# A retention branch projected per head as seven block products, its heads summed in memory token by token

## The chip, the cores and the metric

The kernel runs on one core of a Trainium2 chip. The metric is the device time of one execution in microseconds; lower is better. The core has TensorE (PE in the profile; PEld is its weight load), VectorE (DVE), ScalarE (ACT), GpSimd (POOL) and SyncE (SP). In this kernel SP and POOL issue nearly all DMAs: SP the plain loads, POOL the stores and the DMAs that add to what is in their destination.

## The reference

One decoder layer on 512 tokens of width 1024. A retention branch and a latent attention branch read the same normalised input; each is projected to width 1024 and gated; their sum goes through an output projection into the residual. An MLP and a gated embedding follow. Cut to the branch in question:

```python
rv = rv.reshape(B, S, RET_HEADS, RET_V_DIM)            # 4 heads, 512 values each
ro = retention(rq, rk, rv)
ro = rms_norm(ro, ret_norm.reshape(RET_HEADS, RET_V_DIM)).reshape(B, S, RET_V_W)
a_ret = (ro * jax.nn.silu(rg)) @ w_br                  # (512 x 2048) @ (2048 x 1024)
...
mixed = jax.nn.sigmoid(gr) * a_ret + jax.nn.sigmoid(gm) * a_mla
x = x + mixed @ w_o
```

The norm's factor is one number for each token and head. As `a_ret` is linear in each head, a head's factor may be applied ahead of `w_br` or behind it, and the four heads' shares may be summed in any order.

## The kernel before

All matrices are handled in tiles of 128 partitions. Every operand of a matmul is held as two tiles, a rounded high part and the low remainder, and each product is three matmuls (`mm3`, line 291). `split` (line 301) makes the two parts: a copy on ACT, then a subtraction on DVE. Weights come as chunks of 128 x 1024 from one stream: `prepare` (line 217) issues the load into a raw buffer, and `load_chunk` (line 246) converts it with one ACT copy and one DVE subtraction. There are 6 raw buffers and 3 pairs of converted ones.

The work is a list of steps in TensorE's order (from line 1099). `run_steps` (line 270) converts the weights of the step behind the present one and prepares three steps ahead. TensorE's order is the list's; on the other engines a planner orders the instructions by the list's priority and its own estimate of when each is ready. Each engine works through its own queue in order.

**Seven products.** Some projections are cut into 2 x 2 blocks and done as seven block products instead of eight: the values (`ret_v`, two heads at once), the gates (`ret_gate`, per head) and the MLP's second matrix (`down`). For these (`key[0] == "sw"`) the sums of weight blocks are made by DMA: product 7 loads a block into a raw buffer t and adds another to it with an accumulating DMA from POOL (line 223); once t is converted, product 6 adds a third block to the same t, and product 4 later a fourth. Product 5 is a load and an accumulation in a buffer of its own; products 1, 2 and 3 are plain loads. Products accumulate in PSUM along three chains (`CHAIN`, line 735): 1, 6, 5, 3 on one; 7, 4 on another; 2 alone. The bank is read behind each product, and the next product of the chain is added on top.

**A head of the retention.** The list from line 1195 has, for each of four heads: queries and keys in four steps (`ret_qk`); for heads 0 and 2 the values of this head and the next (14 steps); the gates in seven steps with `ret_scores`, `ret_attend` and `ret_stats` between them; then `ret_gated`, which multiplies the head's output (features on partitions, tokens along the row) by the gate. `ret_factor` (line 847) comes in the following head, behind its first query step: it spreads the norm's factor over the partitions with four transposes (the tile pbo), multiplies the four tiles by it and splits them. Then `branch_r` (line 855) multiplies by `w_br`: 4 chunks a head, each for two of the eight 128-wide slices of the output, with the weights as the stationary operand and the tokens as the 512 columns. Heads 1 and 3 do their own steps around the branch of the head before; in head 2 the branch of head 1 lies between the values' products.

The result of head 0 is stored in memory (`aside`, line 351); those of heads 1 and 2 are added to it by accumulating DMAs from POOL (line 865). Behind the last head, `reload` (line 869) brings the sums, the gated attention share (zm) and the output gates (sgr) back; the rest of the gates is computed (`gate_r`); head 3's branch is added by DVE directly from PSUM (line 867); and `mix` (line 894) gates, adds and splits each of eight tiles for the output projection `wo`.

**Buffers.** `T` gives one of 45 tiles of 128 x 512 (line 55, NDYN), `K` one of 16 longer-lived ones, `B` one of 8 PSUM banks. During the retention 12 of the K tiles hold the operands of products 6, 5 and 3 of the normalised input. The attention's rotary tiles qp have six buffers of their own (line 567).

## Time and profile before

| | us |
|---|---|
| time, median of 3 runs | 1123.46 (1120.56 to 1124.0) |
| time of the profiled execution | 1125.78 |
| span of the profiled execution, first to last instruction | 1124.0 |
| mean granted TensorE clock in it | 0.997 |

A matmul of 512 columns shows as 389 ns on PE, but matmuls overlap: from start to start they are nearer to the pace that the chain of work shows. Busy PE is therefore no measure of its speed, but idle PE is time lost. The chain of work is followed back from the last instruction to what released each step, so a DMA or an ACT copy on it stands for a stretch in which TensorE was waiting or had no time in hand. From the page, the stretches of the span by engine on that chain, and three groups of DMA issues that the change bears on (destination and source, issuer, count, size, median us from issue to landing):

```profile
PE 87%; DVE 4%; DMA 4%; ACT 2%; issue 2%; SPq 0%; ACTq 0%; DVEq 0%; POOLq 0%
...
wr_rg<-wstream SPq DMA_DIRECT2D x20, 512.0 KB, 4.6
...
wr_rg<-wstream POOLq DMA_DIRECT2D x16, 512.0 KB, 7.7
wr_br<-wstream SPq DMA_DIRECT2D x16, 512.0 KB, 3.5
```

A plain load of a weight chunk lands 3.5 to 4.6 us behind its issue; an accumulating one of the same size takes 7.7.

### The profile page before, as it was taken

To read this page: it belongs to the slowest core of one execution; us is meant where nothing else is said; L and a number is where in the kernel's file an instruction comes from. 1 tells how busy PE (TensorE), PEld (TensorE's weight loads), DVE (VectorE), ACT (ScalarE), POOL (GpSimd) and SP (SyncE) were. 2 spreads that over 40 slices of the span, in tenths; PEclk is the share of its full clock that TensorE was granted. 3 is DMA by queue.
4 is the path that set the end of the run, shared out by engine and by line. 5 is a ranking of instruction groups with operands and counts; after the bars stand their busy time and mean duration, and the time that the engine had idled before them with its cause. 6 is when DMAs were issued, how large, how long until landed. Compare 5 with 4: busy or idle time off the path is not lost.

```text
span 1124.0 us, 14722 instructions
## 1 busy us (share of the span) xinstructions
PE 1107.5 (99%) x5549; PEld 939.0 (84%) x5549; DVE 734.9 (65%) x1206; ACT 536.7 (48%) x762; POOL 85.4 (8%) x113
## 2 busy tenths in 40 slices
PE   9999999999999999999999999999999999999998
PEld 7878878888888889888888987888888888888877
DVE  7777677556785836845483678555466666668675
ACT  7457556444465435445443644434443443445542
POOL 0000000001110020031003000010100100101000
PEclk9999999999999999999999999999999999999999
DMA  8133231356786274599529754693855755738501
GB/s 264 59 98 106 67 99 57 128 210 211 190 225 173 87 212 121 135 202 253 137 92 220 223 172 154 196 274 117 171 165 168 176 166 155 186 123 219 146 29 75
DMA packets 59223, 175.97 MB, mean 157 GB/s; under 512 B 7248, under 2 KB 8656, under 8 KB 58896
## 3 DMA queue, kind: packets, MB, share of 16 engines
q1 hardware_dynamic: 45168, 129.66, 33.8%
q0 software_dynamic: 13840, 45.36, 20.9%
q8 instruction: 43, 0.70, 0.2%
q14 instruction: 28, 0.23, 0.1%
q10 hardware_dynamic: 144, 0.03, 0.0%
HBM read 156.92 MB, written 15.99 MB: 154 GB/s over the span
## 4 chain that ended last, share of the span: by engine, by line
PE 87%; DVE 4%; DMA 4%; ACT 2%; issue 2%; SPq 0%; ACTq 0%; DVEq 0%; POOLq 0%
PE up L168 16%; PE dn L168 14%; PE br L168 6%; PE rg L168 5%; PE rv L168 5%; PE pg L168 4%; PE gr L168 4%; PE rq L168 4%; PE rk L168 4%; PE bm L168 4%; PE wo L168 4%; DMA wr_rg<-wstream 4%; PE gm L168 3%; PE ro L168 3%; PE sc L168 2%
## 5 line engine op out<-in xcount | busy, mean ns | idle before, releaser
L168 PE MATMUL dn<-wh_dn,cl 128*128 128x512 f32 x224 | 87.2, 389 | 0.0
L168 PE MATMUL dn<-wh_dn,ch 128*128 128x512 f32 x224 | 87.2, 389 | 0.0
L168 PE MATMUL dn<-wl_dn,ch 128*128 128x512 f32 x224 | 87.1, 389 | 0.0
L261 ACT ACTIVATE wh_dn<-wr_dn 128x1024 fp32r<-128x1024 f32 x32 | 34.0, 1062 | 75.5 <-PE up L168 54.3
L261 ACT ACTIVATE wh_up<-wr_up 128x1024 fp32r<-128x1024 f32 x32 | 33.9, 1061 | 57.4 <-PE up L168 29.3
L265 DVE TENSOR_TENSOR wl_dn<-wr_dn,wh_dn 128x1024 fp32r<-128x1024 f32 x32 | 39.0, 1220 | 27.5 <-ACT wh_dn L261 27.5
L265 DVE TENSOR_TENSOR wl_rg<-wr_rg,wh_rg 128x1024 fp32r<-128x1024 f32 x20 | 24.3, 1223 | 40.7 <-ACT wh_rg L261 40.4
L265 DVE TENSOR_TENSOR wl_up<-wr_up,wh_up 128x1024 fp32r<-128x1024 f32 x32 | 39.1, 1222 | 17.4 <-ACT wh_up L261 17.4
L970 DVE SCALAR_TENSOR_TENSOR f<-up,bcx 128x512 f32<-128x512 f32 x32 | 20.6, 685 | 44.1 <-PE up L168 44.1
L168 PEld LDWEIGHTS dn<-wl_dn,ch 128*128 128x128 f32 x224 | 42.0, 188 | 8.8
L168 PEld LDWEIGHTS dn<-wh_dn,cl 128*128 128x128 f32 x224 | 42.0, 188 | 8.7
L168 PEld LDWEIGHTS dn<-wh_dn,ch 128*128 128x128 f32 x224 | 42.0, 188 | 8.6
L261 ACT ACTIVATE wh_dn<-dr_dn 128x1024 fp32r<-128x1024 f32 x24 | 25.5, 1060 | 42.2 <-PE up L168 29.1
L223 POOL DMA_DIRECT2D dr_dn<-wstream x24 | 21.4, 892 | 306.3 <-DMA dr_dn<-wstream 182.0
L265 DVE TENSOR_TENSOR wl_dn<-dr_dn,wh_dn 128x1024 fp32r<-128x1024 f32 x24 | 29.3, 1222 | 22.4 <-ACT wh_dn L261 22.4
L261 ACT ACTIVATE wh_rv<-wr_rv 128x1024 fp32r<-128x1024 f32 x28 | 29.6, 1058 | 28.7 <-PE rv L168 11.8
L261 ACT ACTIVATE wh_rg<-wr_rg 128x1024 fp32r<-128x1024 f32 x28 | 29.3, 1054 | 28.9 <-DMA wr_rg<-wstream 23.6
L265 DVE TENSOR_TENSOR wl_br<-wr_br,wh_br 128x1024 fp32r<-128x1024 f32 x16 | 19.5, 1219 | 21.6 <-ACT wh_br L261 21.6
L1028 DVE TENSOR_TENSOR d<-d,dn 128x1024 f32<-128x1024 f32 x24 | 29.2, 1219 | 6.5 <-PE dn L168 6.5
L265 DVE TENSOR_TENSOR wl_rv<-wr_rv,wh_rv 128x1024 fp32r<-128x1024 f32 x20 | 24.4, 1223 | 13.6 <-ACT wh_rv L261 13.6
L861 ACT ACTIVATE rt<-br 128x512 f32<-128x512 f32 x24 | 14.3, 596 | 36.1 <-PE br L168 30.9
L644 ACT ACTIVATE p<-p,ng,hr 128x128 f32<-128x128 f32 (+3 forms) x32 | 20.6, 646 | 15.6 <-DVE ng L642 15.5
(1820 smaller groups left out, 3618.9 us busy)
## 6 DMA issues: line engine op xcount, KB each, us to landing
wr_up<-wstream SPq DMA_DIRECT2D x32, 512.0 KB, 4.4
wr_dn<-wstream SPq DMA_DIRECT2D x32, 512.0 KB, 3.4
dr_dn<-wstream POOLq DMA_DIRECT2D x24, 512.0 KB, 7.6
wr_rv<-wstream SPq DMA_DIRECT2D x20, 512.0 KB, 4.1
wr_rg<-wstream SPq DMA_DIRECT2D x20, 512.0 KB, 4.6
wr_rv<-wstream POOLq DMA_DIRECT2D x16, 512.0 KB, 6.1
wr_rg<-wstream POOLq DMA_DIRECT2D x16, 512.0 KB, 7.7
wr_br<-wstream SPq DMA_DIRECT2D x16, 512.0 KB, 3.5
```

The lines of the kernel that those rows point to most:

```text
L168: return tc.keep_in_program_order(nc.tensor.matmul(*a, **k))
L223: nc.gpsimd.dma_start(raw, chunk(("w", blk, kb, fb, c)), accum_op=ALU.add)
L261: i = ACT(hi, raw, AF.Copy, scale=sign)
L265: TT(lo, raw, hi.bitcast(F32), op=ALU.subtract)
L644: ACT(cols[b], cols[b], AF.Exp, bias=ng[:, b:b + 1], scale=d["rq"][:, b], accum_out=sums[:, b:b + 1])
L861: ACT(t, ps, AF.Copy)
L970: STT(u[:, i], ps[:, i], 0.0, V["bcx2"], op0=ALU.max, op1=ALU.mult)
L1028: TT(to, to, dps[p], op=ALU.add if sign > 0 else ALU.subtract)
```

## The change

Each head's branch becomes seven block products. The roles are exchanged: the head's gated output is the stationary operand and the weights are the 512 columns, so the result has tokens on partitions and the output's width along the row. In this layout the norm's factor is one number per partition. It is applied as the scale of the ACT copy that reads PSUM (or, in the last head, of a DVE operation that also adds), with its negative (`nr`) for products 1, 6 and 4. `ret_factor` with its four transposes and multiplications goes.

The weights of a head are four blocks (256 rows x 512 columns each) used as for the other seven-product projections: 5 plain loads and 4 accumulations, 7 conversions. The output tiles are now 128 tokens x 512 and there are eight of them, `ret[b, n]`: four token blocks by two halves of the width. Head 0 stores the results of products 1, 7, 6 and 3 and accumulates those of 2, 5 and 4; heads 1 and 2 accumulate all 14; head 3 adds all 14 on DVE to the reloaded sums.

`branch_operand` makes a product's operand: a difference where the product needs one, then a split. Those of products 1 and 7 are asked for behind the head's gates, the others two products ahead. The products lie between the next head's query and key steps, in all heads.

Since the sums have tokens on partitions, `ret_turn` transposes each of the eight final tiles once, as four 128 x 128 transposes, for the mix.

Buffers: the values of heads 1 and 3 are stored in memory and loaded back (`odd_v`); the head's output is in two tiles with a tag of their own (o2); qp moves into the common ring, which grows from 45 to 47; result tiles come from K; the reloaded output gates come from T.

```diff
-NDYN, NKEEP, NW, NRAW, NDRAW, AHEAD, PREP, EARLY, PAD = 45, 16, 3, 6, 4, 1, 3, 5, 104
+NDYN, NKEEP, NW, NRAW, NDRAW, AHEAD, PREP, EARLY, PAD = 47, 16, 3, 6, 4, 1, 3, 5, 72
...
+                add(("w", ("br", h), kb, fb, 0), "w_br", _rng(h * RV + kb * 256, 256), _rng(fb * S, S))
...
-            t = dyn.tile([P, S], F32R, tag="qp", name=f"qp{gq}{i}", bufs=6)
+            t = dyn.tile([P, S], F32R, tag="t", name=f"qp{gq}{i}")
...
+                    if blk % 10 == 1:
+                        v[j] = split(t, f"rv{q}{blk}{i}")
+                        continue
+                    if blk == 12:
+                        t = T(f"cv{q}{i}_12")
+                        ACT(t, rvps[ch][i], AF.Copy)
+                    v[j] = aside(f"v{q}{j}", t)
+
+    def odd_v(h):
+        for j in range(4):
+            t = T(f"cv{h}{j}")
+            nc.sync.dma_start(t, R[h]["v"][j])
+            R[h]["v"][j] = split(t, f"rv{h}{j}")
...
+        R[h]["nr"] = sm(f"nro{h}", keep=True)
+        TS(R[h]["nr"], R[h]["r"], -1.0, None, op0=ALU.mult)
...
-    def ret_factor(h):
-        d, r = R[h], R[h]["r"]
-        bc = bcast(B(f"pbo{h}"), lambda b: r[:, b:b + 1])
-        for m in range(4):
-            TT(d["og"][m], d["og"][m], bc, op=ALU.mult)
-            new = K if m < 2 and h < RH - 1 else T
-            d["rog"][m] = split(d["og"][m], None, hi=new(f"rog{h}{m}h", F32R), lo=new(f"rog{h}{m}l", F32R))
...
+    def branch_operand(h, p):
+
+        (a, b), lo_, hi_ = R[h]["o"], slice(0, 256), slice(256, 512)
+        if p == 7:
+            R[h]["s"] = T(f"bs{h}")
+        sv = two(R[h]["s"]) if "s" in R[h] else None
+        if p in (1, 2, 4):
+            src = (a if p == 1 else b)[:, :, hi_ if p == 4 else lo_]
+        elif p == 5:
+            src = two(T(f"bt{h}"))
+            TT(src, a[:, :, hi_], b[:, :, hi_], op=ALU.subtract)
+        else:
+            src = sv
+            if p == 7:
+                TT(sv, a[:, :, hi_], a[:, :, lo_], op=ALU.subtract)
+            else:
+                TT(sv, b[:, :, hi_ if p == 6 else lo_], sv, op=ALU.subtract)
+        hi, lo = two(T(f"bx{h}{p}h", F32R)), two(T(f"bx{h}{p}l", F32R))
+        split(src, None, hi=hi, lo=lo)
+        R[h]["x", p] = [(hi[:, k], lo[:, k]) for k in range(2)]
...
+    def branch_r(w, h, p):
+
+        ch, d = CHAIN[p], R[h]
+        if p in (1, 7, 2):
+            brps[ch] = [B(f"br{h}{p}{i}") for i in range(2)]
+        for k in range(2):
+            for i in range(2):
+                mm3(brps[ch][i], cut(d["x", p][k], i * P), cut(w, k * S, S), p in (1, 7, 2) and k == 0, k == 1,
+                    skip_group_check=True)
+        to, f = {1: (11, "nr"), 7: (22, "r"), 6: (21, "nr"), 2: (11, "r"), 5: (22, "r"), 4: (21, "nr"), 3: (12, "r")}[p]
         for i in range(2):
...
+            b, n = 2 * (to // 10 - 1) + i, to % 10 - 1
+            r, ps = d[f][:, b:b + 1], brps[ch][i]
+            if h == RH - 1:
+                STT(ret[b, n], ps, r, ret[b, n], op0=ALU.mult, op1=ALU.add)
+                continue
+            t = K(f"rt{h}{p}{i}")
+            ACT(t, ps, AF.Copy, scale=r)
+            if h == 0 and p in (1, 7, 6, 3):
+                ret[b, n] = aside(f"ret{b}{n}", t)
             else:
-                TT(ret[n], ret[n], ps, op=ALU.add)
+                nc.gpsimd.dma_start(ret[b, n], t, accum_op=ALU.add)
...
+    def ret_turn(n):
+
+        trp[n] = B(f"tr{n}")
+        for b in range(4):
+            MM(trp[n][:, b * P:b * P + P], ret[b, n // 4][:, n % 4 * P:n % 4 * P + P], ident, is_transpose=True,
+               start=b == 0, stop=b == 3, skip_group_check=True)
...
-        TT(ret[n], ret[n], sgr[n], op=ALU.mult)
-        TT(ret[n], ret[n], zm[n], op=ALU.add)
-        mixed[n] = split(ret[n], f"mix{n}")
+        TT(sgr[n], trp[n], sgr[n], op=ALU.mult)
+        TT(sgr[n], sgr[n], zm[n], op=ALU.add)
+        mixed[n] = split(sgr[n], f"mix{n}")
...
+        qk("rq", 0)()
+        if h:
+            branch_steps(h - 1, [1, qk("rq", 1), 7, 2, qk("rk", 0), 6, 5, qk("rk", 1), 3, 4])
...
+        if h % 2:
+            step(None, odd_v, h)
...
         step(None, ret_gated, h)
+        for p in (1, 7):
+            step(None, branch_operand, h, p)
+    step(None, ret_back)
     for n in range(8):
         step(None, reload, n)
...
+    step(("gr", 5), gate_r, 5)
+    branch_steps(RH - 1, [1, 7, lambda: step(("gr", 6), gate_r, 6), 2, 6, 5, 4, 3])
+    for n in range(4):
+        step(None, ret_turn, n)
+        step(None, mix, n)
+    step(("gr", 7), gate_r, 7)
+    for n in range(4, 8):
+        step(None, ret_turn, n)
+        step(None, mix, n)
```

`ret_back` is eight loads on SP into K tiles; `branch_steps` lists the products and asks for each operand two products ahead.

76 lines of the change are left out of this document (35 added, 41 removed).

## The prediction

> **What bounds the kernel now.** I read the busy times first, then the chain of work that ended last, then the windows of the retention stage. The page's busy times, and from its third part the two large DMA queues:
>
> ```profile
> PE 1107.5 (99%) x5549; PEld 939.0 (84%) x5549; DVE 734.9 (65%) x1206; ACT 536.7 (48%) x762; POOL 85.4 (8%) x113
> ...
> q1 hardware_dynamic: 45168, 129.66, 33.8%
> q0 software_dynamic: 13840, 45.36, 20.9%
> ```
>
> TensorE is idle for only 1124.0 - 1107.5 = 16.5 us of the span. So a matmul less is time won, as long as everything that feeds TensorE stays ahead of it. The chain of work that ended last (start, length, what) gives the pace of the pieces that the change touches; the last but two lines are from the same chain, asked for the end of head 3:
>
> ```profile
> 396.97 21.76 PE br L168 x96
> ...
> 1060.83 1.75 PE tr L168 x16
> ...
> 647.36 5.46 PE gr L168 x24
> 652.82 0.44 PE pbo L168 x4
> ```
>
> 96 matmuls of 512 columns take 21.76 us, so one takes 0.2267 us. Sixteen 128x128 transposes take 1.75 us, so one takes 0.109 us. The four transposes that spread a head's factor (pbo) hold TensorE for 0.44 us. Where TensorE did wait, in the middle of heads 0 and 2, the chain of head 0 reads:
>
> ```profile
> 324.66 4.58 DMA wr_rg<-wstream
> 329.79 8.53 DMA wr_rg<-wstream
> 338.43 1.07 ACT wh_rg L261
> 339.52 1.24 DVE wl_rg L265
> 341.04 6.83 DMA wr_rg<-wstream
> ```
>
> This is one raw weight buffer used four times in series: a load, an accumulating DMA for product 7, a conversion on ACT and DVE, the accumulating DMA for product 6, and so on. The windows (us; busy of PE, PEld, DVE, ACT, POOL with counts; clock; DMA share; GB/s) show what surrounds it:
>
> ```profile
> 322.80:359.00 36.20, 34.57 (x204) 30.45 (x203) 24.21 (x32) 18.28 (x27) 3.44 (x4) 1.00 0.76 203
> 451.40:485.00 33.60, 33.60 (x151) 27.79 (x150) 25.15 (x42) 14.92 (x20) 4.31 (x5) 1.00 0.59 145
> 485.00:540.00 55.00, 55.00 (x267) 46.51 (x266) 27.49 (x29) 26.62 (x35) 12.10 (x14) 1.00 0.98 238
> 540.00:553.40 13.40, 10.84 (x80) 10.23 (x78) 8.35 (x14) 7.08 (x12) 0.86 (x1) 1.00 0.38 96
> 380.60:418.70 38.10, 38.10 (x171) 31.52 (x170) 22.41 (x31) 15.74 (x22) 6.47 (x10) 1.00 0.57 169
> 645.00:692.00 47.00, 46.45 (x216) 38.54 (x215) 38.68 (x65) 19.93 (x28) 0.00 (x0) 1.00 0.45 149
> ```
>
> TensorE loses 36.20 - 34.57 = 1.6 us in head 0 and 13.40 - 10.84 = 2.6 us in head 2, the latter after 55 us in which the DMA engines were at 0.98. So the retention stage is bound by TensorE, with the DMA engines close behind in the even heads, and DVE close behind at the very end (38.68 of 47 us).
>
> **The change part by part.** Durations are of the profiled execution (span 1124.0, its own time 1125.78); the sum is a difference, and I apply it to the median 1123.46.
>
> *Products.* A head's branch took 8 outputs x 4 x 3 = 96 matmuls of 512 columns. Seven products of 2 x 2 x 3 make 84. Four heads: 48 x 0.2267 = **-10.9 us**. The pbo transposes go: 4 x 0.44 = **-1.8**. The turn adds 8 x 4 transposes at 0.109: **+3.5**. TensorE alone: **-9.1 us**. All of it is on the path, since nothing hides a busy TensorE. The Trainium skill (TensorE: Matmul & The Clock Gate, Wait — 56ns, not 53.3ns?) gives 215.7 ns between warm matmuls of 512 columns; this trace has 226.7 at a granted clock of 1.00, and the trace decides. By the page the first term would be -10.4.
>
> *Waits between products.* Product 5 accumulates onto the banks of product 6 directly behind it, so its first matmuls wait until both banks are read. The same turn stands once in the trace, in the value projection (TensorE's timeline):
>
> ```profile
> 322.63 0.39 PE L168 MATMUL rv<-wh_rv,s61h 128*128 128x512 f32 x1
> 323.03 0.51 PE L168 MATMUL rv<-wh_rv,s50l 128*128 128x512 f32 x1
> 323.55 0.50 PE L168 MATMUL rv<-wl_rv,s50h 128*128 128x512 f32 x1
> 323.89 0.39 PE L168 MATMUL rv<-wh_rv,s50h 128*128 128x512 f32 x1
> ```
>
> Three steps took 1.26 us instead of 0.68: 0.58 us. Four heads: **+2.3**. Bounds: 0 (copies at once, the gap being something else) and 5 (two reads behind a 1.07 us conversion each time). A late conversion of wl_rv ends at the same place, so the row is an upper reading for ACT; in head 3 DVE does the reading and is fuller.
>
> *Operands and conversions.* Per head three more weight blocks are converted (1.07 ACT, 1.24 DVE), six more results leave PSUM, the four multiplications by the factor go, and there are seven splits and four differences instead of four splits. In heads 1 to 3 the queries and keys that now lie between the products had 22.41 us of DVE in 38.10 (380.60 to 418.70); with 3 x 1.14 for conversions, and some 2 to 4 us for operands and the second head's values, some 29 in 35. TensorE covers it, 5.44 us for each rq or rk step. If that cover went, 7 us per head would show; I take 0.
>
> *The end.* Here DVE decides. Its timeline:
>
> ```profile
> 649.86 1.22 DVE L265 TENSOR_TENSOR wl_gr<-wr_gr,wh_gr 128x1024 fp32r<-128x1024 f32 x1
> ...
> 676.99 1.22 DVE L265 TENSOR_TENSOR wl_o<-wr_o,wh_o 128x1024 fp32r<-128x1024 f32 x1
> 678.12 0.68 DVE L307 TENSOR_TENSOR mix2l<-re,mix2h 128x512 fp32r<-128x512 f32 x1
> 678.73 0.68 DVE L898 TENSOR_TENSOR re<-re,ze 128x512 f32<-128x512 f32 x1
> 679.33 0.68 DVE L867 TENSOR_TENSOR re<-re,br 128x512 f32<-128x512 f32 x1
> ...
> 691.40 0.68 DVE L307 TENSOR_TENSOR mix7l<-re,mix7h 128x512 fp32r<-128x512 f32 x1
> ```
>
> From start to start a 512-wide operation takes 0.60 us, a conversion 1.14. From 649.9 to the last mix at 692 DVE had 4 + 4 + 8 + 24 operations of 0.60 and 8 conversions of 1.14: 33 us in 42. After the change: 7 splits and 4 differences, 14 accumulations, 24 of the mix (49 x 0.60) and 12 conversions (13.7): 43 us. TensorE reaches the matmul that needs the last mix at 647.36 + 3 x 5.44 + 7 x 2.72 + 3.5 + 5.44 + 2.0 = 693.7, so DVE has 43.8 us for 43, and each instruction that it waits for counts. It sat idle for 9 us before; I allow 3, hence **+2.5** (0 to 6). Behind a DVE that waits stand the splits that the next product needs.
>
> *DMA.* The rates come from the queue rows: 129.66 MB in 0.338 x 1124 us of all sixteen engines is 1.54 us per 512 KB load. On q0 29 plain stores of 256 KB at that pace are 22 us of 235; the other 37.7 MB are accumulating, 2.95 us per 512 KB. A head's branch now needs 5 loads and 4 accumulations instead of 4 loads (+13.3 us), and 14 results for memory instead of 8 (+8.9 where all accumulate); an even head also stores four value tiles (+3.1). Head 2 gets 25.3 us more. From 451.4 to 553.4 the engines were free for 0.41 x 33.6 + 0.02 x 55 + 0.62 x 13.4 = 23 us. So it is nearly full, and the serial chain of the gate weights at its end, which already stalls, becomes later: **+1.5** in head 0 (the value stores fall on it) and **+1.5** in head 2. Bounds 0 and 9 together: none of it in the way, or head 2 full and late by 5.4 us (25.3 less 23, plus the 3.1 that TensorE saves) with 3.1 from the stores in head 0. The result tiles have 4 of 16 keep buffers (12 hold the operands of products 6, 5 and 3), each reused after two products and one rq or rk step of TensorE (2 x 2.72 + 5.44 = 10.9 us). Their DMAs (issue rows of the rt tile):
>
> ```profile
> L861 ACT ACTIVATE rt<-br x24: 580/598/600, 400.1 to 614.8; 128x512 f32<-128x512 f32 x24
> ...
> DMA to landing us min/median/max: 2.3/6.2/10.6
> ```
>
> 0.6 + 0.9 of issue + 6.2 fits; the maximum doesn't, by 1.2 us. When it doesn't, ACT stands at the copy with the conversions behind it, and on POOL the weights' accumulations queue behind the results'. **+1.5** for heads 1 to 3 (0 to 6). The Trainium skill (DMA: Bandwidth & Descriptors, Issuing engines are not separate DMA queues) says that DMAs of all issuers run on the same 16 engines and interleave. That speaks against the change: the accumulations on POOL would not be beside SP's loads but among them. By it the sum is at worst that of the DMA rival below; were POOL's queue a way of its own, the 3.0 and 1.5 of this part would be 0. The 0.98 of 485 to 540, where both queues ran, fits the Trainium skill's sentence.
>
> *Attention.* qp moves from 6 buffers of its own into the common ring, 45 to 47, where 4 or more qp live: two fewer for the rest. The ring was full once (DVE's waits, 45 to 236 us):
>
> ```profile
> DVE o L557 <- DMA zm5d<-zm: 2.2, 1, 2.2
> ```
>
> **+0.5** (-1 to 3). *Reloads.* SP's 8 loads of the sums stand ahead of those of zm, 16 keep buffers for 16 tiles instead of 21; weights queued behind them wait no longer than before: 0 (-1 to 1).
>
> **Sum:** -9.1 + 2.3 + 2.5 + 3.0 + 1.5 + 0.5 = +0.7 us, so **1124 us**: what TensorE saves is given back in small waits.
>
> **The rivals.** *Faster:* the waits are hidden. For it: 55 us at a DMA share of 0.98 passed without one PE stall, and raw buffers run several steps ahead. Then the 6-to-5 wait and one or two us at the end remain: -9.1 + 2.3 + 1.8 = -5, **1118.5**; with nothing at all, 1114. *Slower, by DMA:* in head 2, from the first branch product to the last gate product, accumulations of results and of weights share POOL's queue and the engines. It decides once the DMA share stays at 1.0 beyond 540: 5.4 us late in head 2, 3.1 in head 0 and some 2 each in heads 1 and 3 in place of the 4.5 taken: +9, **1132**. Against it: result tiles aren't urgent. *Slower, by DVE at the end:* if DVE idles 9 us there as before, mixes come 8 us late: 5.5 more than taken, **1130**. *The saving isn't there:* the products are fewer by count, so only a slower matmul could do this; no row suggests it.
>
> **How the numbers follow.** Forecast, no change: 0.38, 1120 to 1127. Faster: 0.32. Slower by DMA: 0.19; slower by DVE at the end: 0.11. A measurement of this kernel tells about 0.3% (3.4 us) from no change; faster is below 1120.1, slower above 1126.8. Range 1113 (nothing in the way) to 1134 (one slow case with a little of the other).
>
> **What would show it.** Right: 5549 - 48 + 16 = 5517 matmuls, PE busy near 1098, PE idle grown by some 10 us at the 6-to-5 turns, the gate products of heads 0 and 2, and ahead of wo. Wrong: idle as before (16 us) means that the waits were hidden; DMA waits inside the branch products mean the DMA rival; a span grown in 45 to 236 us means that the ring of tiles mattered.

## The result: 5% slower, and the profile after

| | before | after |
|---|---|---|
| time, median of 4 runs (us) | 1123.73 | 1181.9 (1180.92 to 1183.23) |
| ratio to before, 95% interval | | 1.0522 (1.0497 to 1.0547) |
| span of the profiled execution (us) | 1124.0 | 1180.0 |
| mean granted TensorE clock in it | 0.997 | 0.978 |

The forecast was 1124 us, with a range from 1113 to 1134. The change costs 58 us.

From the page of the kernel after, the busy times and the two large DMA queues:

```profile
PE 1108.7 (94%) x5517; PEld 935.3 (79%) x5517; DVE 761.1 (64%) x1224; ACT 567.9 (48%) x808; POOL 120.6 (10%) x155
...
q1 hardware_dynamic: 46896, 133.85, 33.4%
q0 software_dynamic: 19376, 60.56, 26.8%
```

The 5517 matmuls are those that were foreseen. TensorE was idle for 16.5 us before; now it is idle for 1180.0 - 1108.7 = 71.3 us. That is 54.8 of the 56.0 us by which the span grew. The other 1.2 us hide two things that nearly cancel. The work got 9.1 us less, by the prediction's count, so busy PE should have come to 1098.4; the remaining 10.3 us are matmuls that took longer at a lower granted clock. They show where the count did not change. All matmuls of the gates (first line, tile rg) and of the output projection (second line, tile wo), us and count behind the length of the window, then granted clock, DMA share and GB/s; before:

```profile
0.00:1200.00 1200.00, 83.50 (x672) 1.00 0.52 147
...
0.00:1200.00 1200.00, 43.98 (x192) 1.00 0.52 147
```

and after:

```profile
0.00:1200.00 1200.00, 88.25 (x672) 0.98 0.60 163
...
0.00:1200.00 1200.00, 46.25 (x192) 0.98 0.60 163
```

The same 672 matmuls take 4.75 us more and the same 192 take 2.27 more; with the values (tile rv, 77.71 to 81.27) that makes 10.6 us.

What TensorE waited for longest, after (tile it was about to write, who released it; us in total, times, longest):

```profile
PE rg L167 <- ACT z L741: 34.4, 2, 17.6
PE rv L167 <- ACT wh_rv L260: 4.6, 1, 4.6
PE wo L167 <- DVE wl_o L264: 4.6, 1, 4.6
```

Two waits are the larger half of the loss: 34.4 us, in the gates of heads 1 and 3. Product 6 of a gate adds onto the banks of product 1, so it must wait until ACT has copied them out (the tile z). No such row stood in the kernel before. Why is a copy of 0.6 us late by 17 us? ACT's timeline of head 1, after, answers it (start, length, line, what, and in brackets the idle time ahead of it with its releaser):

```profile
420.82 0.69 ACT L904 ACTIVATE rt<-br,nro 128x512 f32<-128x512 f32 x1 [4.47 <-DMA ret21d<-rt]
423.00 0.69 ACT L904 ACTIVATE rt<-br,nro 128x512 f32<-128x512 f32 x1 [1.49 <-DMA ret31d<-rt]
423.59 1.05 ACT L260 ACTIVATE wh_rg<-wr_rg 128x1024 fp32r<-128x1024 f32 x1
424.54 0.62 ACT L305 ACTIVATE rv10h<-cv 128x512 fp32r<-128x512 f32 x1
433.86 1.06 ACT L260 ACTIVATE wh_rg<-wr_rg 128x1024 fp32r<-128x1024 f32 x1 [8.70 <-DMA wr_rg<-wstream]
434.82 0.61 ACT L305 ACTIVATE rv11h<-cv 128x512 fp32r<-128x512 f32 x1
435.34 1.04 ACT L260 ACTIVATE wh_rg<-wr_rg 128x1024 fp32r<-128x1024 f32 x1
436.29 0.61 ACT L305 ACTIVATE rv12h<-cv 128x512 fp32r<-128x512 f32 x1
442.06 1.06 ACT L260 ACTIVATE wh_rg<-wr_rg 128x1024 fp32r<-128x1024 f32 x1 [5.16 <-DMA wr_rg<-wstream]
444.65 0.63 ACT L305 ACTIVATE rv13h<-cv 128x512 fp32r<-128x512 f32 x1 [1.53 <-DMA cv<-v03d]
445.18 1.07 ACT L741 ACTIVATE z<-rg 128x512 f32<-128x512 f32 x2
```

The rows show a queue in which one urgent instruction stands last. TensorE had finished product 2 by 429 and needed z. But the planner had put z behind the splits of the reloaded values (rv10h to rv13h), and between these lie the conversions of the gate's products 6, 5 and 4. Two of the conversions and the last split wait for transfers (8.70, 5.16 and 1.53 us), so ACT stood still, with z in its queue. In the kernel before, the two copies stood directly behind the conversions of products 2 and 6, and nothing that waits for a transfer came between; ACT's timeline of head 1, before:

```profile
419.31 1.05 ACT L261 ACTIVATE wh_rg<-wr_rg 128x1024 fp32r<-128x1024 f32 x1
421.69 0.60 ACT L742 ACTIVATE z<-rg 128x512 f32<-128x512 f32 x1 [1.33 <-issue]
422.19 1.05 ACT L261 ACTIVATE wh_rg<-wr_rg 128x1024 fp32r<-128x1024 f32 x1
424.52 0.60 ACT L742 ACTIVATE z<-rg 128x512 f32<-128x512 f32 x1 [1.29 <-PE rg L168]
```

The first of these transfers was late itself. POOL's timeline in the same stretch, after:

```profile
421.81 0.89 POOL L908 DMA_DIRECT2D ret20d<-rt  x1 [6.07 <-ACT rt L904]
423.99 0.87 POOL L908 DMA_DIRECT2D ret30d<-rt  x1 [1.29 <-ACT rt L904]
424.55 1.22 POOL L222 DMA_DIRECT2D wr_rg<-wstream  x1
436.47 0.86 POOL L222 DMA_DIRECT2D wr_rg<-wstream  x1 [10.70 <-DVE wl_rg L264]
```

The sum of weights for product 6 (424.55) was issued behind two accumulations of results. These waited for ACT's copies at 420.82 and 423.00, which had waited for a free result tile, that is, for earlier accumulations to land (4.47 and 1.49 us, first lines of ACT's rows). So one late tile passed through three queues.

What a long wait costs beyond itself, in windows of 10 us, after (length; busy and count of PE, PEld, DVE, ACT, POOL; clock; DMA share; GB/s), and TensorE's first matmuls behind it:

```profile
430.00:440.00 10.00, 0.00 (x0) 0.00 (x0) 3.56 (x4) 3.04 (x4) 0.86 (x1) 0.62 0.50 121
440.00:450.00 10.00, 4.18 (x22) 4.19 (x23) 5.64 (x10) 4.01 (x7) 0.86 (x1) 0.53 0.71 185
```

```profile
427.12 0.28 PE L167 MATMUL rg<-xn7h,wl_rg 128*128 128x256 f32 x1
427.24 0.28 PE L167 MATMUL rg<-xn7l,wh_rg 128*128 128x256 f32 x1
...
445.81 0.58 PE L167 MATMUL rg<-s60h,wl_rg 128*128 128x256 f32 x1 [16.74 <-ACT z L741]
446.19 0.41 PE L167 MATMUL rg<-s60l,wh_rg 128*128 128x256 f32 x1
446.41 0.41 PE L167 MATMUL rg<-s60h,wh_rg 128*128 128x256 f32 x1
```

Ahead of the wait a matmul of 256 columns started every 0.12 us; behind it one every 0.21 to 0.22, at a granted clock of 0.53. The Trainium skill (TensorE: Matmul & The Clock Gate, What's actually happening) says that an idle window of about 3.4 us brings the clock to half; this trace agrees, with 0.53 behind an idle time of 16.74 us. In the same trace 4.60 us were enough: behind the wait for wl_o in the list above, matmuls of 512 columns started every 0.43 us (742.24, 742.67), and later every 0.23 (747.36, 747.59).

### The profile page after: what moved, and what is told of

The parts are those of the page before. It is cut to its first block, busy times and chain, and to the rows that moved or that the text cites. A ratio compares the mean times of both kernels' runs of the same rounds, so it can differ in the third digit from the quotient of the medians.

```text
span 1180.0 us, 14846 instructions
## 1 busy us (share of the span) xinstructions
PE 1108.7 (94%) x5517; PEld 935.3 (79%) x5517; DVE 761.1 (64%) x1224; ACT 567.9 (48%) x808; POOL 120.6 (10%) x155
## 5 line engine op out<-in xcount | busy, mean ns | idle before, releaser
L260 ACT ACTIVATE wh_br<-wr_br 128x1024 fp32r<-128x1024 f32 x28 | 29.6, 1058 | 21.2 <-DMA wr_br<-wstream 12.5
L167 PE MATMUL rg<-s60h,wl_rg 128*128 128x256 f32 x16 | 5.9, 367 | 34.4 <-ACT z L741 34.4
L167 PEld LDWEIGHTS rg<-s60h,wl_rg 128*128 128x128 f32 x16 | 4.1, 256 | 34.8 <-ACT z L741 34.8
```

The costliest lines, as they stand in the source:

```text
L167: return tc.keep_in_program_order(nc.tensor.matmul(*a, **k))
L260: i = ACT(hi, raw, AF.Copy, scale=sign)
```

## The experiments

The theories at the start. **Order:** instructions that TensorE waits for stand in ACT's and DVE's queues behind ones that wait for transfers, because the planner fixes the order ahead of time. **Transfers:** the added traffic fills the DMA engines, and everything comes late, in whatever order. **Tiles:** result tiles and attention tiles share too few buffers. **End:** DVE's work between the last product and the output projection. The first four runs:

*1. The values of heads 1 and 3 asked for earlier, ahead of the head's first query step.*

```diff
+        if h % 2:
+            step(None, odd_v, h)
         qk("rq", 0)()
...
-        if h % 2:
-            step(None, odd_v, h)
```

> The reload and split of an odd head's values (odd_v) is listed ahead of the head's first query step instead of behind its last key step. Theory Q (order of ACT's queue): in heads 1 and 3 the copies of the first gate products (z) stand in ACT's queue behind the conversions of gate products 6, 5, 4 and behind the values' splits; with the step moved they stand ahead of them. Q expects the two waits of 17 us of PE rg for ACT z (34.4 us together) to fall under 2 us each, the granted clock to stay at 1.00 there (about 8 us more), and a time of 1137 to 1146. Theory D (the DMA engines are full, and TensorE would wait for the gate weights anyway): the wait moves from z to the conversions of rg, and the time stays above 1165.

1175.66 us, ratio 1.0468 (1.0407 to 1.0529). The waits for z fell to 0.7 us, as the order theory had it, but the time missed its range of 1137 to 1146. TensorE now waited at another place (waits of this run):

```profile
PE br L167 <- DVE bx22l L306: 10.6, 1, 10.6
PE br L167 <- DVE bx02l L306: 7.9, 1, 7.9
```

The operands of product 2 stood behind the values' splits, whose loads were late again (SP issued them behind weight loads that waited for raw buffers). The wait moved with the splits, and not to the gate weights, where the theory of transfers put it. That speaks for order; but the time is above 1165, where that theory put it too, so moving the splits settles little.

*2. Heads 1 and 3 use the values of the head before; the reload and the splits are left out, the stores stay.*

```diff
-            step(None, odd_v, h)
+            step(None, lambda h=h: R[h].update(v=R[h - 1]["v"]))
```

> Heads 1 and 3 use the values of the head before, so their reload (8 loads) and their splits are left out; the stores of the values stay. Q expects the same as with the step moved, 1135 to 1145, as nothing of the step stands in ACT's queue. If the reload itself (its DMAs, ACT and DVE work) were the cost rather than its place, this is faster than the moved step by more than 10 us. D expects above 1165.

1157.06 us (one run). No wait for z is left, but 15.0 us of waits of gate products for their weights (wl_rg), two of them long, both at product 6 of heads 1 and 3. That is the second half of the mechanism, the sums behind the results in POOL's queue, without the first. The time lies in neither expected range, and 18.6 us below run 1: by the expectation, what costs is the reload itself with its splits, and not only its place.

*3. The 28 accumulating transfers of heads 1 and 2 are left out, the values are as in the changed kernel.*

```diff
-            else:
+            elif h == 0:
                 nc.gpsimd.dma_start(ret[b, n], t, accum_op=ALU.add)
```

> The 28 accumulating DMAs of the results of heads 1 and 2 are left out (so their shares are missing from the sum); everything else, the values' step included, stays. Theory D expects the waits of 17 us in heads 1 and 3 to go in head 3 (whose stage carries head 2's results), stay in head 1 (head 0's results are still stored), and head 2's idle in 500 to 550 us (about 14 us with the slow clock) to go: 1140 or less. Q alone expects head 3's wait to stay at 10 us or more, as ACT's order is the same, and the time at 1160 to 1175.

1169.18 us (one run), waits for z still 27.6 us. Without these 28 transfers most of the long waiting stays, as the order theory expected, so they are not its main cause. They cost some 12 us all the same. The waits for z are 6.8 us shorter, and in head 2, from 500 to 560 us, TensorE is 5.0 us busier, in the changed kernel first and then in this run:

```profile
500.00:560.00 60.00, 52.75 (x214) 41.33 (x213) 29.20 (x33) 27.30 (x36) 16.93 (x20) 0.94 1.01 243
```

```profile
500.00:560.00 60.00, 57.74 (x268) 47.65 (x267) 31.56 (x34) 29.76 (x38) 10.88 (x14) 0.97 0.89 222
```

In that stretch the DMA engines of the changed kernel are full (1.01) and TensorE is idle for 7.25 us: there the theory of transfers holds.

*4. The kernel before, with only the attention's qp tiles moved into the common ring of 47.*

```diff
-NDYN, NKEEP, NW, NRAW, NDRAW, AHEAD, PREP, EARLY, PAD = 45, 16, 3, 6, 4, 1, 3, 5, 104
+NDYN, NKEEP, NW, NRAW, NDRAW, AHEAD, PREP, EARLY, PAD = 47, 16, 3, 6, 4, 1, 3, 5, 104
...
-            t = dyn.tile([P, S], F32R, tag="qp", name=f"qp{gq}{i}", bufs=6)
+            t = dyn.tile([P, S], F32R, tag="t", name=f"qp{gq}{i}")
```

> The kernel before with one part of the change alone: qp in the common ring, which goes from 45 to 47 tiles. From 45 to 236 us TensorE idled about 3 us longer in the changed kernel. If the ring is the cause, this is 2 to 5 us slower than before; if that came from elsewhere (another plan of the order), within 1 us.

1127.95 us, ratio 1.0033 (1.0007 to 1.0058): by that ratio the ring alone costs 3.7 us. The window from 50 to 250 us of the kernel before, and of this one:

```profile
50.00:250.00 200.00, 195.45 (x1082) 166.06 (x1081) 140.14 (x374) 112.28 (x226) 7.77 (x14) 1.00 0.33 107
```

```profile
50.00:250.00 200.00, 192.18 (x1059) 163.12 (x1058) 136.44 (x368) 108.78 (x222) 7.23 (x13) 0.99 0.33 101
```

TensorE loses 3.3 us there, and as much in the changed kernel (192.11 busy).

*5 to 8, one set.* First the values split at once and kept, with nothing left out; then the same with the result tiles taken from the common ring:

```diff
-                    if blk % 10 == 1:
-                        v[j] = split(t, f"rv{q}{blk}{i}")
-                        continue
...
-                    v[j] = aside(f"v{q}{j}", t)
+                    v[j] = split(t, f"rv{q}{blk}{i}")
...
-        if h % 2:
-            step(None, odd_v, h)
```

> The values of heads 1 and 3 are split at once and kept on the chip, as in the kernel before; nothing else is taken back. If ScalarE's order decides (the values' splits ahead of the gate's result copies in its queue), the two long waits of the gate in heads 1 and 3 fall from 34.4 to below 5 us, and a wait of gate products for their weights of about 13 us stays, as when heads 1 and 3 used the values of the head before: 1152 to 1162. If it is only the work of the values (loads and splits) and not its place, the same time. If the two waits come from transfers and not from the order, they stay: 1170 to 1180. If the kept values crowd the common ring, new waits on its tiles: over 1165.

```diff
-            t = K(f"rt{h}{p}{i}")
+            t = T(f"rt{h}{p}{i}")
```

> As the run with the values kept, and the scaled block results are taken from the common ring of 47 tiles in place of the kept ones, of which 4 are free. If the gate weights' sums are late because POOL's queue holds accumulations of results that wait for one of those 4 buffers, the wait of gate products for their weights (13.6 us in two places) falls below 4: 10 to 14 below the run with the values kept, 1142 to 1150. If they are late because the transfers themselves fill the DMA engines, no more than 3 below it. If the ring gets short, other operands come late and it is slower than it.

Kept values: 1164.44 us, ratio 1.0376 (1.0323 to 1.0428). With the results in the ring too: 1150.12, ratio 1.0265 (1.0217 to 1.0313). The first wait is from the run with the values kept, the next two from the run with both:

```profile
PE rg L167 <- DVE wl_rg L264: 13.3, 3, 7.7
```

```profile
PE br L167 <- ACT bx33h L305: 5.6, 1, 5.6
...
PE br L167 <- ACT rt L898: 4.5, 4, 2.5
```

Keeping the values removes the waits for z (a ratio 0.0146 lower, some 16 us). More result tiles remove the waits for gate weights, 13.3 to 0.5 us (0.0111, some 12 us). The waits went as the order theory and its chain through POOL said; the time of run 5 lies 2.4 us above its range of 1152 to 1162.

Run 5 shows the order at work in head 1, on ACT and then on TensorE:

```profile
424.49 0.59 ACT L741 ACTIVATE z<-rg 128x512 f32<-128x512 f32 x1
433.93 1.06 ACT L260 ACTIVATE wh_rg<-wr_rg 128x1024 fp32r<-128x1024 f32 x1 [8.85 <-DMA wr_rg<-wstream]
```

```profile
436.30 0.58 PE L167 MATMUL rg<-s60h,wl_rg 128*128 128x256 f32 x1 [4.96 <-DVE wl_rg L264]
```

The conversion of product 6's weights starts when it did in the changed kernel (433.86), but product 1's z now stands ahead of it, and no split is there to hold z back. TensorE resumed at 436.30, once the weights were converted, and not at 445.81. So of the 16.74 us some 9.5 were the place of z, and the rest the late weights, which run 6 shortened.

*7. The values asked for later, behind gate products 1 and 7.*

```diff
         for p in (1, 7):
             step(("sw", ("rg", h), p, 0), ret_gate, h, p)
+        if h % 2:
+            step(None, odd_v, h)
```

The step is taken out where it stood.

> The values are still stored and loaded again, but loaded and split behind gate products 1 and 7 in place of ahead of them. If ScalarE's order decides, the gate's result copies no longer stand behind the splits, the long waits go, and the time falls to 1155 to 1168 (loads and splits are all still there, and they must be done before the attended products of the head). If the amount of work decides, it stays at 1176 to 1186.

1186.42 us, ratio 1.0585 (1.053 to 1.064): the order theory's range, 1155 to 1168, is missed, and the time is just above the range for the amount of work, 1176 to 1186. The waits for z went, as expected, but others came:

```profile
PE ro L167 <- ACT ath L305: 25.2, 2, 13.9
PE rg L167 <- DVE wl_rg L264: 17.0, 4, 8.1
```

Now the attended scores (ath) stand behind the last split of the values, which waits for its load. I had counted only on what the splits no longer block. With runs 1 and 7 the splits have stood in three places, and each time the instruction behind them was late by 8 to 18 us. Their work is no reason for that, as the four splits of a head keep ACT busy for 2.5 us; the long part is the wait for their loads. No place was found for them. Keeping the values, which takes away loads and splits together, is what helps.

*8. Shared values (as in 2) and no accumulations of heads 1 and 2 (as in 3).*

> Heads 1 and 3 use the values of the head before (their reload and splits are left out), and the 28 accumulating result transfers of heads 1 and 2 are left out. Against the run that shares the values alone (1157.1): if the remaining 15.0 us of waits for gate weights come from result transfers ahead of the weights' sums in POOL's queue, they go, 1141 to 1147; if they come from the load of the DMA engines by weights, less than 5 us: 1152 to 1157. What is left above the kernel before (1123.5) is then the attention's ring (3.7 measured), the end of the program and the slower clock behind waits: some 15 to 20 us.

1145.58 us (one run), 11.5 below run 2 and in the first expectation's range. The two are from different sets, in which the kernel before took 1124.32 and 1120.27; as ratios they are some 7 us apart. The waits for gate weights fell from 15.0 to 6.2 us, not to nothing: so the results ahead of them seem to be more than half of it.

*9 to 12, all on the version of run 6 (ratio 1.0265).* In run 9 plain stores, issued by ACT, take the place of the 28 accumulations:

```diff
-            else:
+            elif h == 0:
                 nc.gpsimd.dma_start(ret[b, n], t, accum_op=ALU.add)
+            else:
+                nc.scalar.dma_start(spill.tile([P, S], F32, tag=f"rt{h}{p}{i}", name=f"rt{h}{p}{i}d"), t)
```

> On the version with kept values and results in the common ring (1150.1, 1.0265 of the kernel before). The 28 accumulating transfers of the results of heads 1 and 2 become plain stores of the same bytes, each into a place of its own, issued by ScalarE behind its copies: the sum over heads lacks heads 1 and 2. If the bytes on the DMA engines make the remaining waits around 500 to 550 and 600 to 620 us, the ratio stays, 1.023 to 1.029. If it is that the sums go through POOL's queue, or that accumulating takes longer on the engines than storing, it falls to 1.012 to 1.021.

In run 10 the two results that go to the same block are added on the chip:

```diff
-            t = T(f"rt{h}{p}{i}")
-            ACT(t, ps, AF.Copy, scale=r)
-            if h == 0 and p in (1, 7, 6, 3):
+            if p in (2, 5, 4):
+                t = d["f", {2: 1, 5: 7, 4: 6}[p], i]
+                STT(t, ps, r, t, op0=ALU.mult, op1=ALU.add)
+            else:
+                t = d["f", p, i] = T(f"rt{h}{p}{i}")
+                ACT(t, ps, AF.Copy, scale=r)
+                if p != 3:
+                    continue
+            if h == 0:
```

> On the same version: the two results of a head that go to the same block (products 1 and 2, 7 and 5, 6 and 4) are added by VectorE before they leave, so heads 1 and 2 accumulate 16 tiles in memory in place of 28 and head 0 none in place of 6. Nothing is left out. If the traffic or the queue of the sums costs what leaving them out gave (about 11 us for 28), 18 fewer give 5 to 8: ratio 1.019 to 1.023. If the longer life of the result tiles or VectorE's 18 more instructions decide, it is 1.025 to 1.035.

Run 9: 1151.05 us, ratio 1.025 (1.0217 to 1.0282), no change. Run 10: 1138.71, ratio 1.0141 (1.0095 to 1.0187). The same transfers without POOL's queue and without the adding take the same time, in the range expected if the bytes are the cost. But the stores now stand in ACT's queue, most of them for 0.33 us each, so a gain may be hidden by that. Fewer of them do help, by more than expected (0.0124, some 14 us against 5 to 8). What fewer transfers bring together, less traffic, fewer tiles waiting to land and 18 fewer copies on ACT, these runs don't tell apart. The wait of products for ACT's result copies, 4.5 us above, is below 0.4 in run 10.

In run 11 the reloads come later, and run 12 has both edits:

```diff
-    for n in range(8):
-        step(None, reload, n)
-    step(("gr", 5), gate_r, 5)
-    branch_steps(RH - 1, [1, 7, lambda: step(("gr", 6), gate_r, 6), 2, 6, 5, 4, 3])
+    def back(a, b):
+        return lambda: [step(None, reload, n) for n in range(a, b)]
+
+    step(("gr", 5), gate_r, 5)
+    branch_steps(RH - 1, [1, 7, lambda: step(("gr", 6), gate_r, 6), 2, back(0, 3), 6, back(3, 8), 5, 4, 3])
```

> On the same version: the reloads of the gates and of the attention's mix are asked for behind the last head's products 2 and 6 in place of ahead of its product 1, so that ScalarE's sigmoids no longer stand, waiting for them (5.4 us at 675), ahead of the weights and operands of the last branch. If that wait is what makes the last head's products wait (5.6 us for bx33h) the ratio falls by 0.003 to 0.006, to 1.021 to 1.024. If VectorE's work between the last product and the output projection sets the end of this stage, the wait only moves behind and the ratio stays within 1.025 to 1.029.

> Both of the two edits before. If they act in different stretches, their gains add up: ratio 1.012 to 1.020. If one covers the other's wait, 1.019 to 1.025. In no case as fast as the kernel before: the attention's ring (3.7) and the output projection's start (4.6 and the slower clock behind it) are untouched.

Run 11: 1149.59 us, ratio 1.024 (1.0198 to 1.0282); the 5.6 us wait for bx33h is gone, but other waits remain and the interval overlaps that of run 6. Run 12: 1132.99, ratio 1.0093 (1.0064 to 1.0122), below the expected 1.012 to 1.020, and lower than run 10 by 0.0048 (the intervals overlap a little), about the wait that went, 5.7 us for bx33h in run 10. It is the same pattern once more: ACT's sigmoids of the reloaded gates waited 5.3 us for a load, with the weights and operands of the last products behind them.

*13 to 18.* Run 13 puts half of the mixes beside the last products (on run 12; `turned(a, b)` lists `ret_turn` and `mix` for the tiles from a to b), and run 14 moves the query tiles to pair buffers as well, by the edit shown with run 16. In runs 13, 14 and 15 the last head's product 6 is made with weights that already hold those of product 4: in the new order that sum went ahead of product 6's conversion. The amount of work is the same, but product 6 now waits for one transfer more.

```diff
-    branch_steps(RH - 1, [1, 7, lambda: step(("gr", 6), gate_r, 6), 2, back(0, 3), 6, back(3, 8), 5, 4, 3])
...
+    branch_steps(RH - 1, [1, 7, lambda: step(("gr", 6), gate_r, 6), 2, back(0, 3), 6, back(3, 8), 4, lambda: turned(0, 4), 5, 3])
+    step(("gr", 7), gate_r, 7)
+    turned(4, 8)
```

> On the version with kept values, folded sums and late reloads (1133.0, 1.0093 of the kernel before). The last head's product 4 is taken ahead of 5 and 3, and the first four transposed blocks with their mixes stand behind it, so that half of VectorE's work between the last product and the output projection lies beside products 5 and 3 and the last gate. If VectorE's work there sets the end of the stage, the 4.6 us wait of the output projection falls below 1.5 and the slower clock behind it goes: 1126 to 1130, ratio 1.002 to 1.006. If the end is set by the weights of the output projection, it stays at 1.007 to 1.012. If the mixes now stand ahead of the operands of product 3 in VectorE's queue, a wait for bx33 takes its place and the ratio is 1.008 to 1.013.

> As the version with the early turn, and the attention's six query tiles leave the common ring (45 tiles again) for three pairs that the retention's outputs use later. If the attention's part of the loss is the shared ring (1127.95 against 1124.3 measured alone, 3.7), the stretch from 50 to 250 us is 2 to 4 shorter and the ratio is 0.002 to 0.004 below the run before it, 0.999 to 1.003: no slower than the kernel before. If the shorter ring costs the retention as much as it gives, the ratio is that of the run before it within 0.002.

Run 13: 1136.39 us, ratio 1.0118 (1.009 to 1.0145). Run 14: 1133.21, ratio 1.0105 (1.0072 to 1.0138), not the 0.999 to 1.003 expected of it, and no measurable gain on run 13. The output projection's wait went and another took its place (run 13's waits):

```profile
PE br L167 <- DVE re L895: 5.5, 1, 5.5
```

Product 3 waited for DVE to read product 5's banks, and that sum stood behind the mixes in DVE's queue. This is the third expectation of run 13, by range and by cause, though for another instruction than bx33. Run 15 takes the mixes behind that sum, in the order 1, 7, 2, 6, 4, 5, the gate 6, four mixes, 3, with the four transposed blocks in the banks of products 2 and 7. Run 16 has the query pairs alone, on run 12:

```diff
-NDYN, NKEEP, NW, NRAW, NDRAW, AHEAD, PREP, EARLY, PAD = 47, 16, 3, 6, 4, 1, 3, 5, 72
+NDYN, NKEEP, NW, NRAW, NDRAW, AHEAD, PREP, EARLY, PAD = 45, 16, 3, 6, 4, 1, 3, 5, 72
...
-            t = dyn.tile([P, S], F32R, tag="t", name=f"qp{gq}{i}")
+            if i % 2 == 0:
+                qp2 = dyn.tile([P, 2, S], F32R, tag="o2", name=f"qp{gq}{i}", bufs=3)
+            t = qp2[:, i % 2]
...
-        d["o"] = [dyn.tile([P, 2, S], F32, tag="o2", name=f"og{h}{k}", bufs=2) for k in range(2)]
+        d["o"] = [dyn.tile([P, 2, S], F32, tag="o2", name=f"og{h}{k}", bufs=3) for k in range(2)]
```

> The early turn again, on the version with the query tiles in pairs, with the mixes out of the way of the block sums: products in the order 1, 7, 2, 6, 4, 5, then the gate 6 ahead of product 3, the first four transposed blocks (into the banks of products 2 and 7) and their mixes behind the gate, then product 3 and the gate 7. Nothing is left out. If the 5.5 us that product 3 waited in the run before came from the mixes standing ahead of product 5's sum in VectorE's queue, that wait falls below 1 and the 4.6 us wait of the output projection does not come back: ratio 0.999 to 1.004. If the gate 6 is missed where it stood (behind product 7), products 2 and 6 wait for their operands instead, 2 to 5 us: ratio 1.003 to 1.008.

> Only the query tiles in pairs, on the version with kept values, folded sums and late reloads (1.0093). If the attention's shared ring costs 3 to 4 us, the stretch from 50 to 250 us is as full as in the kernel before (195.4 of 200 us against 192.1) and the ratio is 1.004 to 1.008. If the two tiles fewer in the ring cost the retention as much, it stays at 1.008 to 1.011.

Run 15: 1128.28 us, ratio 1.0056 (1.0028 to 1.0084), in the second expectation's range. The wait for product 5's sum is gone and that of the output projection is down to 0.4 us, but product 6 waited 6.0 us for its weights, which in this order wait for product 4's sum too; so what the mixes would gain alone stays open. Run 16: 1125.3, ratio 1.0028 (1.0004 to 1.0051), below the expected 1.004 to 1.008. Its window from 50 to 250 us:

```profile
50.00:250.00 200.00, 195.41 (x1080) 166.01 (x1079) 140.56 (x374) 111.94 (x226) 8.12 (x15) 1.00 0.34 107
```

195.41 against 195.45 in the kernel before: the attention's loss was the shared ring, and it is back. The step from run 12, some 7 us, is larger than that loss of 3.7, but the two ratios are from different sets and each is known to some 3 us. Run 17 is the early turn with the gate 6 between products 6 and 4; run 18 has run 16's order and one edit in the mix:

```diff
-        TT(sgr[n], sgr[n], zm[n], op=ALU.add)
+        nc.gpsimd.tensor_tensor(sgr[n], sgr[n], zm[n], op=ALU.add)
```

> The version with kept values, folded sums, late reloads and query tiles in pairs (1125.3, 1.0028), with the last head in the order 1, 7, 2, 6, the gate 6, 4, 5, then the first four transposed blocks with their mixes, 3 and the gate 7. Nothing is left out; product 6 has its own weights, since the gate stands between its conversion and the sum of product 4's. If VectorE's mixes set the end of the stage, the 4.6 us wait of the output projection falls to 0 to 2 and nothing takes its place: ratio 0.997 to 1.001. If products 2 and 6 wait for their operands and weights without the gate ahead of them, 2 to 5 us: ratio 1.001 to 1.006.

> The same version (1.0028) with the old order and one edit: the second of the two adds of each mix (with the attention's part) goes from VectorE to GpSimd, 8 of 16 instructions of 0.69 us each. If VectorE's instructions set the end, the output projection's wait of 4.6 us falls to 1 to 3: ratio 0.998 to 1.002. If GpSimd takes over a microsecond and a half for one, the mixes come no earlier and the wait stays or grows: ratio 1.003 to 1.012.

Run 17: 1129.98 us, ratio 1.0063 (1.0038 to 1.0088), above both of its ranges and no faster than run 16, with 4.3 us of wait for wl_o still there. DVE's timeline says why:

```profile
695.41 0.68 DVE L957 TENSOR_TENSOR gr<-gr,ze 128x512 f32<-128x512 f32 x1
696.01 1.22 DVE L264 TENSOR_TENSOR wl_o<-wr_o,wh_o 128x1024 fp32r<-128x1024 f32 x1
```

The first half of the second output tile needs mixes 0 to 3, which were long done, and ACT had done its part of the weights' conversion by 689.37. But DVE's part stood at 696.01 in its queue, behind the mixes of the second half, and TensorE resumed at 697.28. The conversion is short; its place made it late. Run 18: 1122.22, ratio 0.9989 (0.9966 to 1.0012). The wait fell from 4.6 us to this:

```profile
PE wo L167 <- DVE mix6l L306: 1.9, 1, 1.9
```

In this run the planner also moved that conversion forward: DVE made it at 677.77, ahead of mix2l, where in run 16 it stood at 686.83, ahead of mix7l. So the run doesn't tell what the lighter DVE gained from what the new place did.

Run 18 leaves nothing out and is as fast as the kernel before, not measurably faster. Its TensorE was busy for 1098.6 us in a span of 1120.4, at a clock of 0.998.

## Why the prediction was wrong, point by point

The versions that leave nothing out form a ladder, each step one edit on the one above. The ratios are from different sets, so a step is a difference of two, with about the width of their intervals. The planner also orders the queues anew for every edit, so a step is an edit together with what the planner made of it:

| version | ratio to before | step in us (x 1123) |
|---|---|---|
| changed kernel | 1.0522 | |
| values kept (5) | 1.0376 | -16 |
| results in the common ring (6) | 1.0265 | -12 |
| sums folded (10) | 1.0141 | -14 |
| reloads late (12) | 1.0093 | -5 |
| query tiles in pairs (16) | 1.0028 | -7 |
| one add of the mix on GpSimd (18) | 0.9989 | -4 |

- **Products, -9.1 us: right.** 5517 matmuls, and in run 18, where the clock was 0.998, busy PE is 1098.6 against the 1098.4 foreseen.
- **The 6-to-5 waits, +2.3: not there.** No row for these waits stands among those of the changed kernel. The lower bound, 0, held in this kernel. The mechanism is there all the same: in run 6 TensorE waited 4.5 us for copies of results (rt), each time ahead of a product 5.
- **Operands and conversions, 0: this is the step that failed.** The prediction counted "some 2 to 4 us for operands and the second head's values" as DVE work and set the 5.44 us of a query or key step against it. The splits of the values are short indeed (0.62 us each). What they cost is a wait: they stand in the queue until their loads land, and z, bx22 or ath stands behind them. TensorE's cover of 5.44 us is no help there, for the waits were 16.74 and 17.6 us. Measured: 34.4 us of waits with a lower clock behind them, of which keeping the values gave back some 16 us of time; 13.3 us stayed as waits for the sums, next. That z's place makes the difference is shown in head 1 (some 9.5 us, run 5); whether reloaded values could be split anywhere at no cost stays open.
- **DMA.** Head 0's gate chain, +1.5: no such wait (250 to 400 us is full). *Head 2, +1.5: mis-sized.* TensorE was idle for 7.25 us from 500 to 560 with the DMA engines at 1.01, more than the 5.4 that the rival by DMA gave this head. *Result tiles, +1.5 (0 to 6): mis-sized.* The prediction had the mechanism, "ACT stands at the copy with the conversions behind it, and on POOL the weights' accumulations queue behind the results'", but set it against the median landing of 6.2 us. It cost some 12 us, in heads 1 and 3, and folding the sums gave some 14 more. Of the price of the sums' traffic the prediction had 3.0 with a bound of 9 for heads 0 and 2; the rival by DMA, 1132, was nearer in kind and far too small.
- **The end, +2.5 (0 to 6): mis-sized.** The wait for wo is 4.6 us, and it comes with a slower clock behind it; two edits there gave 5 and 4 us, each less than the width of the intervals. Here too a part is order: the reloads' sigmoids ahead of the last operands, and wl_o behind the mixes. *Reloads, 0 (-1 to 1):* wrong, since only SP's queue was looked at and ACT's sigmoid behind the load was not.
- **Attention, +0.5 (-1 to 3): mis-sized.** Measured alone it is 3.7 us (ratio 1.0033).
- **The clock was in no term.** The matmuls behind the long waits ran at a lower granted clock: 10.3 us in the changed kernel.

The range failed because its terms were priced one by one as work on an engine or on the DMA engines, and each was taken from the lower half of its bounds or near it. Even all upper bounds together give no more than -9.1 + 5 + 6 + 9 + 6 + 3 + 1 = 20.9 us, that is some 1144: most of the loss was in no term. Its sign for the rival by DMA, waits for DMA inside the branch products, did not show; the full engines showed in the values' products of head 2. None of the rivals had an urgent instruction standing in an in-order queue behind one that waits for a transfer. The Trainium skill (TensorE: Matmul & The Clock Gate, Architectural detail: the array is 16× 32×32, not 1× 128×128) says that the queues of ScalarE and VectorE are strictly first in, first out; ACT's rows above agree: z, whose products had ended by 429, started at 445.18, directly behind a split that had waited 1.53 us for its load.

## What to carry to other kernels

For each instruction that a change adds to an in-order queue, ask what it waits for and which urgent instruction stands behind it, not how long it takes; here short splits of reloaded data, with the loads that they waited for, cost some 16 us, and the matmuls that were saved were worth 9.1. A long wait of TensorE is paid beyond its length: behind 4.60 us of waiting the matmuls of 512 columns started every 0.43 us, while behind the 1.9 us of run 18 they kept to 0.23. Where results only have to be summed, try adding them on the chip before they travel; that gave some 14 us here. And spilling operands to gain room can cost more than the room is worth, when the reload lands in a busy stretch.

## What the runs showed of the hardware that I had not expected

**VectorE was slower beside GpSimd.** In run 18 DVE's two conversions beside GpSimd's adds took 2.30 us each; the first:

```profile
677.77 2.30 DVE L264 TENSOR_TENSOR wl_o<-wr_o,wh_o 128x1024 fp32r<-128x1024 f32 x1
```

against 1.22 for such a conversion in run 17 (696.01), and again in run 18 once GpSimd was done (694.24). GpSimd's add took 1.28 us at best and 1.74 at most; whether DVE slowed it is not shown. The Trainium skill (GPSIMD Engine Reference, 1. Specifications) says that GpSimd shares its SBUF interfaces with VectorE and contends with VectorE instructions that have two inputs there; the conversion has two, and this trace agrees: an operation of DVE with one of its inputs in PSUM kept to 0.68 us meanwhile (676.07). Even so the wait was shorter.

**Adding in memory took the DMA engines nearly twice as long as storing.** From run 6 to run 9 the queue of POOL lost 7.34 MB and 26.6 - 23.3 = 3.3% of the time of all sixteen engines, about 38 us; the plain stores of the same 7.34 MB took 1.8%, about 21 us. The time of the kernel did not change.
